# Linear attention: three products and the split of the scores on GpSimd, decays multiplied into the queries in place

## The chip, the cores and the metric

One core of one Trainium2 chip. Five engines matter: TensorE (PE in the profile; PEld is its loading of weights), VectorE (DVE), ScalarE (ACT), GpSimd (POOL), and SyncE (SP), which issues the transfers. The metric is the device time of one execution in microseconds; smaller is better.

## The reference

The kernel computes one layer of a hybrid encoder block on 1024 tokens of width 1024. The part that the change touches is branch A, a gated linear attention that runs in both directions, with 4 heads, keys of 128 and values of 256 elements. For one direction:

```python
b = jnp.cumsum(log_g, axis=3)              # within a chunk of 64 tokens
q_dec = q * jnp.exp(b)
k_inv = k * jnp.exp(-b)
k_tail = k * jnp.exp(b_last - b)
scores = jnp.where(mask, einsum(q_dec, k_inv), 0.0)
o_intra = einsum(scores, v)
chunk_kv = einsum(k_tail, v)
state = exp(b_last) * state + chunk_kv     # from chunk to chunk
o_inter = einsum(q_dec, state_before)
```

The backward direction is the same on flipped sequences, without the diagonal. Both results are added, normalised per head and gated. Branch B is a windowed attention with normalised, rotated keys and queries. Both branches go through output projections, a residual and a SwiGLU layer.

## The kernel before

**Precision.** Large products are made from fp32 operands split in two fp32r parts (a high part and a rest), with three matmuls in place of one. A split is a copy on ScalarE and a subtraction on VectorE (`wh` and `wl` of L70 and L72 for the weights; `kth`, `ktl` for turned keys; `sh`, `sl` for scores).

**Stages.** First come projections made with seven products of blocks in place of eight (to about 332 us), then the linear attention (about 332 to 557 us), the windowed attention (about 557 to 735 us), and then output projections and the feed-forward layer.

**The linear attention.** The tokens are handled in chunks of 128 (eight, c = 0 to 7, for each of four heads), and the gates for two chunks at once (a pair, `pr`). Inside a chunk the powers are counted from its middle (element 63), so that a chunk of 128 needs two numbers a direction (`pr.sm`): the log decay from its border to the middle and from the middle to its other border. The functions:

- `g_gates` (every second slot): loads keys and queries `qk`; TensorE makes the gate logits `z`; ScalarE takes exp, VectorE a minimum, ScalarE a logarithm, VectorE the running sum `cs`; `sm` is taken from it.
- `g_powers` (the slot after): `e` is the running sum counted from the middle; two exponentials on ScalarE turn `e` into the powers and the inverse powers (in the tiles `cs` and `e`); four multiplications on VectorE make the keys `en` (two directions) and the queries `q2` (two directions), 128x256 each.
- `g_scores`, two slots after a chunk's number: TensorE turns the keys (`kt`, split into `kth` and `ktl`) and makes the scores of both directions; a ScalarE copy and a VectorE copy under the mask `tri` join them into `sp`, which VectorE splits into `sh` and `sl`.
- `g_out`, four slots after: TensorE makes the keys-times-values `kv` of both directions; a small exponential on ScalarE makes the decay `dec` from the last chunk's middle to this one's; ScalarE scales the state `pf` by it into `th`; VectorE updates the state; TensorE multiplies the scores with the values and adds the query times `th`.
- `g_back_out` and `g_back`: the backward state walks from the last chunk to the first, with its own small exponential and its own scaled copy `thb` on ScalarE; TensorE multiplies the backward query with `thb`; VectorE adds it to the chunk's output `ob`; then come norm and, in `g_turn`, the turn back and the stores.

**What sets the order.** TensorE's order is written out by hand: a loop over slots calls the functions that are due, and between them `fill` issues a number of matmuls of other projections (12 in most slots, 8 later), which need nothing from the linear attention but weights. The other engines run in an order that a planner makes at compile time from the dependences and its own costs of instructions; each engine then runs its list strictly in order. Tiles come from pools with a fixed number of buffers (`bufs`); a tile's next use waits for the readers of the one before. Results of TensorE that these functions read lie in four buffers named `ch`.

Of the kernel before, what the change touches and what calls it, by code (L numbers as in the profile page):

```python
# [8 lines left out]
F32 = mybir.dt.float32  # L9
# [5 lines left out]
P = 128  # L15
# [15 lines left out]
def body(tc, i, out):  # L31
    nc = tc.nc
    with ExitStack() as root:
# [586 lines left out]
        def gtile(tag, shape=(P, 256), dt=F32, bufs=2):  # L620
            return gt.tile(list(shape), dt, tag=tag, name=nm(tag), bufs=bufs)
# [3 lines left out]
        def g_gates(hd, c):  # L625


            pr = Chunk()
            for j in range(2):
                a = gla[hd, c + j] = Chunk()  # L630
                a.pr, a.j, a.t = pr, j, slice(j * P, (j + 1) * P)
            s, co = c // 4, (c % 4) * P
            for nme in ("q", "k"):
                need((f"{nme}{hd}", s))
            qk = gtile("qk", (P, 2, 256))
            nc.sync.dma_start(out=qk[:, 0], in_=scr[f"q{hd}", s][:, co:co + 256])
            nc.sync.dma_start(out=qk[:, 1], in_=scr[f"k{hd}", s][:, co:co + 256])
            if hd == 0:

                r = rstd[:, c * P:(c + 2) * P]  # L640
                nc.vector.scalar_tensor_tensor(qk[:, 0], qk[:, 0], 128 ** -0.5, r, op0=ALU.mult, op1=ALU.mult)
                nc.vector.tensor_tensor(qk[:, 1], qk[:, 1], r, op=ALU.mult)
            z = chtile((P, 2, 256))
            for d in range(2):
                mm(z[:, d], upS[:, d, hd * P:(hd + 1) * P], lrS[:, c * P:(c + 2) * P], True, True)
            e = gtile("e", (P, 2, 2, P), bufs=1)
            ef = e.rearrange("p d j t -> p (d j t)")
            nc.scalar.activation(ef, z.rearrange("p d t -> p (d t)"), AF.Exp, scale=-1.0)

            nc.vector.tensor_scalar(ef, ef, float(np.expm1(8.0)), None, op0=ALU.min)  # L650
            nc.scalar.activation(ef, ef, AF.Ln, bias=ones[:, 0:1])

            cs = gtile("cs", (P, 2, 2, P), bufs=1)
            csf = cs.rearrange("p d j t -> p (d j t)")
            nc.vector.tensor_tensor_scan(csf, mask.rearrange("p c t -> p (c t)"), ef, 0.0, op0=ALU.mult, op1=ALU.add)  # L655

            pr.qk, pr.e, pr.cs = qk, e, cs
            pr.sm = gtile("sm", (P, 2, 2, 2), bufs=16)
            nc.vector.tensor_scalar(pr.sm, cs[:, :, :, 63:128:64], -1.0 / 16, None, op0=ALU.mult)
            nc.vector.tensor_tensor(pr.sm[:, :, :, 1], pr.sm[:, :, :, 1], pr.sm[:, :, :, 0], op=ALU.subtract)  # L660

        def g_powers(hd, c):

            pr = gla[hd, c].pr
            qk, e, cs = pr.qk, pr.e, pr.cs
            ef, csf = (v.rearrange("p d j t -> p (d j t)") for v in (e, cs))
            nc.vector.tensor_tensor(e[:, 0], cs[:, 0], cs[:, 0, :, 63:64].to_broadcast([P, 2, P]), op=ALU.subtract)
            nc.vector.tensor_tensor(e[:, 1, :, 1:P], cs[:, 1, :, 0:P - 1], cs[:, 1, :, 63:64].to_broadcast([P, 2, P - 1]),
                                    op=ALU.subtract)
            nc.vector.tensor_scalar(e[:, 1, :, 0:1], cs[:, 1, :, 63:64], -1.0, None, op0=ALU.mult)  # L670

            x1 = cs.rearrange("p d j t -> p d (j t)")
            x2 = e.rearrange("p d j t -> p d (j t)")
            nc.scalar.activation(csf, ef, AF.Exp, scale=-1.0 / 16)
            nc.scalar.activation(ef, ef, AF.Exp, scale=1.0 / 16)
            pr.en = gtile("en", (P, 2, 256))
            nc.vector.tensor_tensor(pr.en[:, 0], x2[:, 0], qk[:, 1], op=ALU.mult)
            nc.vector.tensor_tensor(pr.en[:, 1], x1[:, 1], qk[:, 1], op=ALU.mult)
            pr.q2 = (gtile("q2f", bufs=3), gtile(f"q2b{c}", bufs=(3, 2, 2, 1)[c // 2]))
            nc.vector.tensor_tensor(pr.q2[0], x1[:, 0], qk[:, 0], op=ALU.mult)  # L680
            nc.vector.tensor_tensor(pr.q2[1], x2[:, 1], qk[:, 0], op=ALU.mult)

        def g_scores(hd, c):

            a = gla[hd, c]
            a.vh = gtile("vh", dt=FR, bufs=3)
            a.vl = gtile("vl", dt=FR, bufs=3)
            for t, nme in ((a.vh, "vh"), (a.vl, "vl")):
                nc.sync.dma_start(out=t.bitcast(F32), in_=scr[f"{nme}{hd // 2}", c][:, (hd % 2) * 256:(hd % 2) * 256 + 256])
            kt = chtile((P, 2, P))  # L690
            for d in range(2):
                nc.tensor.transpose(kt[:, d], a.pr.en[:, d, a.t], ident)
            a.kth = gtile("kth", (P, 2, P), FR, bufs=3)
            a.ktl = gtile("ktl", (P, 2, P), FR, bufs=3)
            nc.scalar.activation(a.kth, kt, AF.Copy)
            nc.vector.tensor_tensor(a.ktl, kt, a.kth.bitcast(F32), op=ALU.subtract)
            sc = chtile((P, 2, P))
            for d in range(2):
                mm(sc[:, d], a.pr.en[:, d, a.t], a.pr.q2[d][:, a.t], True, True)
            sp = gtile("sp", (P, P))  # L700
            nc.scalar.copy(sp, sc[:, 0])
            nc.vector.copy_predicated(sp, tri, sc[:, 1])
            a.sh = gtile("sh", (P, P), FR, bufs=3)
            a.sl = gtile("sl", (P, P), FR, bufs=3)
            nc.vector.tensor_copy(a.sh, sp)
            nc.vector.tensor_tensor(a.sl, sp, a.sh.bitcast(F32), op=ALU.subtract)

        def g_out(hd, c):

            a = gla[hd, c]  # L710
            kv = chtile((P, 2, 256))
            for d in range(2):
                mm3(kv[:, d], a.kth[:, d], a.ktl[:, d], a.vh, a.vl, True, True)
            a.pf = gtile("pf")
            if c:
                pf = gla[hd, c - 1].pf
                dec = gtile("dec", (P, 1))
                p = gla[hd, c - 1]
                nc.scalar.activation(dec, a.pr.sm[:, 0, a.j, 0:1], AF.Exp, bias=p.pr.sm[:, 0, p.j, 1:2])
                th = gtile("th")  # L720
                nc.scalar.activation(th, pf, AF.Copy, scale=dec[:, 0:1])
                nc.vector.scalar_tensor_tensor(a.pf, pf, dec[:, 0:1], kv[:, 0], op0=ALU.mult, op1=ALU.add)
                a.kb = gtile(f"kb{c}", bufs=2 if c < 5 else 1)
                nc.scalar.copy(a.kb, kv[:, 1])
            else:
                nc.vector.tensor_copy(a.pf, kv[:, 0])
                a.kb = None
            o = chtile((P, 256))
            mm3(o, a.sh, a.sl, a.vh, a.vl, True, c == 0)
            if c:  # L730
                mm(o, a.pr.q2[0][:, a.t], th, False, True)
            a.ob = gtile(f"ob{c}", bufs=2 if c < 5 else 1)
            nc.scalar.copy(a.ob, o)

        def g_back(hd, c):

            a = gla[hd, c]
            if c < NC - 1:
                n = gla[hd, c + 1]
                dec = gtile("decb", (P, 1))  # L740
                nc.scalar.activation(dec, a.pr.sm[:, 1, a.j, 1:2], AF.Exp, bias=n.pr.sm[:, 1, n.j, 0:1])
                a.thb = gtile("thb")
                nc.scalar.activation(a.thb, n.kb, AF.Copy, scale=dec[:, 0:1])
                if c:
                    nc.vector.scalar_tensor_tensor(a.kb, n.kb, dec[:, 0:1], a.kb, op0=ALU.mult, op1=ALU.add)

        def g_back_out(hd, c):
            a = gla[hd, c]
            if c < NC - 1:
                o2 = chtile((P, 256))  # L750
                mm(o2, a.pr.q2[1][:, a.t], a.thb, True, True)
                nc.vector.tensor_tensor(a.ob, a.ob, o2, op=ALU.add)
            if c:
                g_back(hd, c - 1)

            if c % 2:
                a.ss = gtile("oss", (P, 2))
            ss = a.ss if c % 2 else gla[hd, c + 1].ss
            sq = gtile("osq", bufs=1)
            nc.scalar.activation(sq, a.ob, AF.Square, accum_out=ss[:, 1 - c % 2:2 - c % 2])  # L760
            if c % 2 == 0:
                rs = gtile("ors", (P, 2))
                rsqrt(rs, ss, 1.0 / 256, EPS, epst, gt, (P, 2), "on")
                for j, v in enumerate((gla[hd, c + 1].ob, a.ob)):
                    nc.scalar.activation(v, v, AF.Copy, scale=rs[:, j:j + 1])
# [771 lines left out]
```

## Time and profile before

| what | value |
|---|---|
| median of three runs | 1645.5 us (1644.73 to 1645.68) |
| the profiled execution | 1645.61 us, its span 1643.8 us |
| PE busy | 1626.0 us (99%) |
| DVE busy | 1251.4 us (76%) |
| ACT busy | 842.6 us (51%) |
| POOL busy | 76.0 us (5%), all but a few constants in the windowed attention |
| granted clock of TensorE | full speed in all slices |

The page gives the busy time of each engine, then 40 slices of the span, the transfers, the chain of work that ended last, and groups of instructions with their count, busy time and mean duration. Other views list the same for one tile, a stretch of time, or the waits of one engine for another. A matmul's record overlaps the next one's, so the busy share of PE hides a part of short waits.

### The profile page before, as it was taken

How to read it: one execution, taken by the hardware profiler on the slowest of the kernel's cores; microseconds unless marked ns; L12 is line 12 of the kernel's file. 1: busy time of each engine (PE TensorE's matmuls, PEld its weight loads, DVE VectorE, ACT ScalarE, POOL GpSimd, SP SyncE). 2: the span in 40 equal slices, each digit the busy share in tenths (PEclk: the TensorE clock that was granted, in tenths of full speed). 3: DMA queues.
4: the chain of work that ended last, by engine and by line, in shares of the span. 5: the costliest groups of instructions: out<-in, count | busy, mean ns of one | idle time of the engine just before them, and what ended most of it. 6: DMA issues, size and time to landing. Idle time of an engine off the chain costs nothing.

```text
span 1643.8 us, 23281 instructions
## 1 busy us (share of the span) xinstructions
PE 1626.0 (99%) x7588; PEld 1346.0 (82%) x7588; DVE 1251.4 (76%) x2559; ACT 842.6 (51%) x1762; POOL 76.0 (5%) x68
## 2 busy tenths in 40 slices
PE   9999999999999989999999999999999999999999
PEld 7888888888888778888888888888888888888887
DVE  8866665589986598867885678887777778779655
ACT  8622224468998666665554557333333333354442
POOL 0000000000000034540000000000000000000000
PEclk9999999999999999999999999999999999999999
DMA  7554334475554633248765544443334443596433
GB/s 238 176 178 148 115 122 135 173 250 173 179 161 129 191 108 97 77 138 280 225 205 175 168 146 145 140 149 109 109 115 147 142 147 129 177 341 193 149 98 119
DMA packets 168010, 262.91 MB, mean 160 GB/s; under 512 B 19324, under 2 KB 52860, under 8 KB 167888
## 3 DMA queue, kind: packets, MB, share of 16 engines
q1 hardware_dynamic: 167888, 261.42, 49.8%
q8 instruction: 60, 0.98, 0.2%
q14 instruction: 62, 0.51, 0.1%
HBM read 187.93 MB, written 73.42 MB: 159 GB/s over the span
## 4 chain that ended last, share of the span: by engine, by line
PE 84%; DVE 9%; ACT 4%; DMA 2%; issue 1%; POOL 1%; SPq 0%; ACTq 0%; DVEq 0%
PE mm L76 23%; PE mm L306 9%; PE mm L308 9%; PE mm L307 9%; PE mm L1350 7%; PE ch L1350 5%; PE ch L76 4%; PE ch L306 4%; PE ch L308 4%; PE ch L307 4%; PE ch L460 3%; PE mm L460 2%; ACT p L956 1%; DVE wl L72 1%; DVE cs L655 1%
## 5 line engine op out<-in xcount | busy, mean ns | idle before, releaser
L298 ACT ACTIVATE wh<-ws 128x512 fp32r<-128x512 f32 x132 | 83.3, 632 | 195.9 <-PE mm L307 102.2
L70 ACT ACTIVATE wh<-wr 128x512 fp32r<-128x512 f32 x202 | 124.9, 626 | 87.4 <-PE mm L76 54.9
L72 DVE TENSOR_TENSOR wl<-wr,wh 128x512 fp32r<-128x512 f32 x202 | 137.7, 686 | 26.8 <-ACT wh L70 26.4
L299 DVE TENSOR_TENSOR wl<-ws,wh 128x512 fp32r<-128x512 f32 x132 | 90.5, 686 | 22.7 <-ACT wh L298 22.6
L298 ACT ACTIVATE wh<-wr 128x512 fp32r<-128x512 f32 x69 | 43.6, 632 | 124.8 <-issue 49.7
L962 POOL TENSOR_SCALAR p<-p,rd 128x384 f32<-128x384 f32 (+1 forms) x64 | 75.8, 1202 | 657.1 <-DMA qr<-sq 587.2
L298 ACT ACTIVATE wh<-a 128x512 fp32r<-128x512 f32 x64 | 40.5, 633 | 91.4 <-PE ch L1350 42.3
L76 PE MATMUL mm<-wh,xl 128*128 128x512 f32 x192 | 83.1, 433 | 0.0
L76 PE MATMUL mm<-wh,xh 128*128 128x512 f32 x192 | 79.6, 415 | 0.0
L76 PE MATMUL mm<-wl,xh 128*128 128x512 f32 x192 | 79.6, 414 | 0.0
L299 DVE TENSOR_TENSOR wl<-a,wh 128x512 fp32r<-128x512 f32 x64 | 44.2, 691 | 43.1 <-ACT wh L298 42.5
L1350 PE MATMUL mm<-hh,wh 128*128 128x512 f32 x176 | 68.5, 389 | 0.0
L1350 PE MATMUL mm<-hl,wh 128*128 128x512 f32 x176 | 68.5, 389 | 0.0
L1350 PE MATMUL mm<-hh,wl 128*128 128x512 f32 x176 | 68.5, 389 | 0.0
L76 PE MATMUL mm<-xl,wh 128*128 128x512 f32 x160 | 64.5, 403 | 0.1
L76 PE MATMUL mm<-xh,wh 128*128 128x512 f32 x160 | 64.4, 403 | 0.2 <-ACT wh L70 0.2
L76 PE MATMUL mm<-xh,wl 128*128 128x512 f32 x160 | 59.2, 409 | 0.0
L1320 DVE TENSOR_TENSOR hl<-hr,hh 128x512 fp32r<-128x512 f32 x75 | 51.4, 685 | 3.7 <-ACT hh L1319 3.7
L1350 PE MATMUL ch<-hh,wh 128*128 128x512 f32 x132 | 51.3, 389 | 0.0
L1350 PE MATMUL ch<-hl,wh 128*128 128x512 f32 x132 | 51.3, 389 | 0.0
L1350 PE MATMUL ch<-hh,wl 128*128 128x512 f32 x132 | 51.3, 389 | 0.0
L76 PE MATMUL mm<-oah,wh 128*128 128x512 f32 x128 | 50.2, 392 | 0.0
(620 smaller groups left out, 5077.7 us busy)
## 6 DMA issues: line engine op xcount, KB each, us to landing
wr<-in_w_fi_dram SPq DMA_DIRECT2D x102, 256.0 KB
wr<-in_w_f_dram SPq DMA_DIRECT2D x80, 256.0 KB
wr<-in_w_t_dram SPq DMA_DIRECT2D x56, 256.0 KB
B<-c SPq DMA_DIRECT2D x44, 256.0 KB
T<-tx SPq DMA_DIRECT2D x44, 256.0 KB
a<-in_w_fo_dram SPq DMA_DIRECT2D x44, 256.0 KB
hr<-T SPq DMA_DIRECT2D x44, 256.0 KB
wr<-in_w_ob_dram SPq DMA_DIRECT2D x32, 256.0 KB
```

The costliest lines, as they stand in the source:

```text
L70: nc.scalar.activation(h, raw, AF.Copy)
L72: nc.vector.tensor_tensor(l, raw, h.bitcast(F32), op=ALU.subtract)
L76: nc.tensor.matmul(o, a, b, start=start, stop=stop)
L298: nc.scalar.activation(h, src, AF.Copy)
L299: nc.vector.tensor_tensor(l, src, h.bitcast(F32), op=ALU.subtract)
L306: nc.tensor.matmul(o, h[:, c], x[kk][0], start=start and kk == 0, stop=False, skip_group_check=True)
L307: nc.tensor.matmul(o, h[:, c], x[kk][1], start=False, stop=False, skip_group_check=True)
L308: nc.tensor.matmul(o, l[:, c], x[kk][0], start=False, stop=kk == nk - 1, skip_group_check=True)
L460: nc.tensor.matmul(ys[m], a[:, c], b, start=f0, stop=f1, skip_group_check=True)
L962: nc.gpsimd.tensor_scalar(p[:, h, :w], p[:, h, :w], rd[:, h:h + 1], None, op0=ALU.mult)
L1320: nc.vector.tensor_tensor(l, r, h.bitcast(F32), op=ALU.subtract)
L1350: nc.tensor.matmul(ys[m], a[:, c], b, start=f0, stop=f1, skip_group_check=True)
```

## The change

It touches only the linear attention.

- The tiles `cs` and `e` (one buffer each) become the halves of one tile `pw` with two buffers.
- The two keys of a pair are made by one 128x512 multiplication on GpSimd instead of two of 128x256 on VectorE (their order in `en` is swapped, and the readers index accordingly). The two queries are made on GpSimd instead of VectorE.
- The split of the scores (`sh`, a copy, and `sl`, a subtraction) moves from VectorE to GpSimd.
- The decays of a pair are made in `g_powers`: two small additions on VectorE (one, for a head's first pair) and one exponential on ScalarE. The small exponentials in `g_out` and `g_back` go.
- Instead of scaling the state into a copy (`th`, `thb`, on ScalarE), the query is multiplied by the decay in place, on VectorE, after the scores have read it. TensorE then multiplies it with the state itself (`pf`, and the next chunk's `kb`).

```diff
-            e = gtile("e", (P, 2, 2, P), bufs=1)
+            pr.w = gtile("pw", (P, 2, 2, 2, P))
+            cs, e = pr.w[:, 0], pr.w[:, 1]
...
-            cs = gtile("cs", (P, 2, 2, P), bufs=1)
...
+            pr.dec = gtile("dec", (P, 2, 2), bufs=16)
+            nc.vector.tensor_tensor(pr.dec[:, 1], pr.sm[:, :, 1, 0], pr.sm[:, :, 0, 1], op=ALU.add)
+            if c:
+                nc.vector.tensor_tensor(pr.dec[:, 0], pr.sm[:, :, 0, 0], gla[hd, c - 1].pr.sm[:, :, 1, 1], op=ALU.add)
+            dc = pr.dec[:, 0 if c else 1:2]
+            nc.scalar.activation(dc, dc, AF.Exp)
...
-            nc.vector.tensor_tensor(pr.en[:, 0], x2[:, 0], qk[:, 1], op=ALU.mult)
-            nc.vector.tensor_tensor(pr.en[:, 1], x1[:, 1], qk[:, 1], op=ALU.mult)
+            nc.gpsimd.tensor_tensor(pr.en, pr.w.rearrange("p a d j t -> p (a d) (j t)")[:, 1:3],
+                                    qk[:, 1:2].to_broadcast([P, 2, 256]), op=ALU.mult)
...
-            nc.vector.tensor_tensor(pr.q2[0], x1[:, 0], qk[:, 0], op=ALU.mult)
-            nc.vector.tensor_tensor(pr.q2[1], x2[:, 1], qk[:, 0], op=ALU.mult)
+            nc.gpsimd.tensor_tensor(pr.q2[0], x1[:, 0], qk[:, 0], op=ALU.mult)
+            nc.gpsimd.tensor_tensor(pr.q2[1], x2[:, 1], qk[:, 0], op=ALU.mult)
...
-            nc.vector.tensor_copy(a.sh, sp)
-            nc.vector.tensor_tensor(a.sl, sp, a.sh.bitcast(F32), op=ALU.subtract)
+            nc.gpsimd.tensor_copy(a.sh, sp)
+            nc.gpsimd.tensor_tensor(a.sl, sp, a.sh.bitcast(F32), op=ALU.subtract)
...
-                dec = gtile("dec", (P, 1))
-                p = gla[hd, c - 1]
-                nc.scalar.activation(dec, a.pr.sm[:, 0, a.j, 0:1], AF.Exp, bias=p.pr.sm[:, 0, p.j, 1:2])
-                th = gtile("th")
-                nc.scalar.activation(th, pf, AF.Copy, scale=dec[:, 0:1])
-                nc.vector.scalar_tensor_tensor(a.pf, pf, dec[:, 0:1], kv[:, 0], op0=ALU.mult, op1=ALU.add)
+                dec = a.pr.dec[:, a.j, 0:1]
+                q = a.pr.q2[0][:, a.t]
+                nc.vector.tensor_scalar(q, q, dec, None, op0=ALU.mult)
+                nc.vector.scalar_tensor_tensor(a.pf, pf, dec, kv[:, 0], op0=ALU.mult, op1=ALU.add)
...
-                mm(o, a.pr.q2[0][:, a.t], th, False, True)
+                mm(o, q, pf, False, True)
...
-                dec = gtile("decb", (P, 1))
-                nc.scalar.activation(dec, a.pr.sm[:, 1, a.j, 1:2], AF.Exp, bias=n.pr.sm[:, 1, n.j, 0:1])
-                a.thb = gtile("thb")
-                nc.scalar.activation(a.thb, n.kb, AF.Copy, scale=dec[:, 0:1])
+                dec = (n if a.j else a).pr.dec[:, 1 - a.j, 1:2]
+                q = a.pr.q2[1][:, a.t]
+                nc.vector.tensor_scalar(q, q, dec, None, op0=ALU.mult)
+                a.after = n.kb
...
-                mm(o2, a.pr.q2[1][:, a.t], a.thb, True, True)
+                mm(o2, a.pr.q2[1][:, a.t], a.after, True, True)
```

More of the change, by code (lines that the diff above doesn't have):

```diff
@@ L691, in g_scores @@
             for d in range(2):
-                nc.tensor.transpose(kt[:, d], a.pr.en[:, d, a.t], ident)
+                nc.tensor.transpose(kt[:, d], a.pr.en[:, 1 - d, a.t], ident)
             a.kth = gtile("kth", (P, 2, P), FR, bufs=3)
@@ L698, in g_scores @@
             for d in range(2):
-                mm(sc[:, d], a.pr.en[:, d, a.t], a.pr.q2[d][:, a.t], True, True)
+                mm(sc[:, d], a.pr.en[:, 1 - d, a.t], a.pr.q2[d][:, a.t], True, True)
             sp = gtile("sp", (P, P))
@@ L739, in g_back @@
                 n = gla[hd, c + 1]
-                dec = gtile("decb", (P, 1))
-                nc.scalar.activation(dec, a.pr.sm[:, 1, a.j, 1:2], AF.Exp, bias=n.pr.sm[:, 1, n.j, 0:1])
-                a.thb = gtile("thb")
-                nc.scalar.activation(a.thb, n.kb, AF.Copy, scale=dec[:, 0:1])
+                dec = (n if a.j else a).pr.dec[:, 1 - a.j, 1:2]
+                q = a.pr.q2[1][:, a.t]
+                nc.vector.tensor_scalar(q, q, dec, None, op0=ALU.mult)
+                a.after = n.kb
                 if c:
-                    nc.vector.scalar_tensor_tensor(a.kb, n.kb, dec[:, 0:1], a.kb, op0=ALU.mult, op1=ALU.add)
+                    nc.vector.scalar_tensor_tensor(a.kb, n.kb, dec, a.kb, op0=ALU.mult, op1=ALU.add)
         def g_back_out(hd, c):
```

## The prediction

> **What bounds the kernel now.** I read the page's busy times first, then the windows of the stage that is changed, then the waits inside it.
>
> ```profile
> PE 1626.0 (99%) x7588; PEld 1346.0 (82%) x7588; DVE 1251.4 (76%) x2559; ACT 842.6 (51%) x1762; POOL 76.0 (5%) x68
> ```
>
> TensorE is the bound everywhere. In a windows row stand the stretch, its length, and the busy time of PE, PEld, DVE, ACT and POOL:
>
> ```profile
> 332.00:557.00 225.00, 222.56 (x1246) 188.09 (x1245) 184.71 (x612) 192.29 (x556) 0.00 (x0) 1.00 0.57 173
> 350.00:470.00 120.00, 118.56 (x692) 100.90 (x690) 116.10 (x408) 105.46 (x311) 0.00 (x0) 1.00 0.58 174
> ```
>
> In the linear attention (332 to 557 us) TensorE shows 225 - 222.56 = 2.44 us of idle time; its instructions and their order do not change. So all that this change can win is time in which TensorE waits, however much work it takes from the others. DVE is at 97% and ACT at 88% from 350 to 470 us, and their lateness is what TensorE waits for. The waits of the stage for PE and its weight loads (engine, line, what it waited for: us in total, times, longest):
>
> ```profile
> PEld ch L76 <- ACT ob L733: 3.5, 6, 0.9
> PE ch L76 <- ACT ob L733: 1.4, 4, 0.5
> PEld ch L771 <- ACT ob L765: 1.3, 2, 0.9
> PEld ch L771 <- DVE ktl L696: 1.3, 2, 0.7
> PEld ch L76 <- DVE ktl L696: 1.3, 4, 0.5
> PEld ch L76 <- ACT kb L724: 1.1, 3, 0.5
> PE ch L771 <- ACT ob L765: 0.5, 1, 0.5
> PE ch L771 <- DVE ktl L696: 0.4, 2, 0.2
> ```
>
> PE itself waits 4 + 1 + 2 = 7 times, 1.4 + 0.5 + 0.4 = 2.3 us, mostly for ACT to empty a buffer of TensorE's results (L733) or to finish a norm (L765). The counted idle is not all. Here is the first of these waits:
>
> ```profile
> 401.95 0.39 PE L76 MATMUL mm<-wh,xh 128*128 128x512 f32 x1
> 402.18 0.40 PE L76 MATMUL mm<-wl,xh 128*128 128x512 f32 x1
> 403.08 0.50 PE L76 MATMUL ch<-lrS,upS 98*128 98x256 f32 x2 [0.50 <-ACT ob L733]
> ```
>
> Such matmuls start 402.18 - 401.95 = 0.23 us apart; this one is followed after 0.90 us, so 0.67 us are lost where 0.50 are counted. Each wait hides 0.17 us. Lost time: 2.44 + 7 x 0.17 = 3.6 us. Weight loads add up to 3.5 + 1.3 + 1.3 + 1.3 + 1.1 = 8.5 us of waiting, most of it under matmuls still running; that is an upper bound for the loss.
>
> **The change part by part.** What it takes away (line, engine, shapes and count | busy us, mean ns):
>
> ```profile
> L721 ACT ACTIVATE th<-pf,dec 128x256 f32<-128x256 f32 x28 | 14.5, 518 | 0.2
> L743 ACT ACTIVATE thb<-kb,decb 128x256 f32<-128x256 f32 x28 | 14.1, 511 | 1.1 <-PE ch L76 1.1
> L719 ACT ACTIVATE dec<-sm 128x1 f32<-128x1 f32 x16 | 4.9, 303 | 0.2 <-DVE sm L660 0.2
> L741 ACT ACTIVATE decb<-sm 128x1 f32<-128x1 f32 x16 | 4.6, 286 | 0.8 <-DVE sm L660 0.7
> L719 ACT ACTIVATE dec<-sm,sm 128x1 f32<-128x1 f32 x12 | 3.5, 294 | 0.2 <-DVE sm L659 0.2
> L741 ACT ACTIVATE decb<-sm,sm 128x1 f32<-128x1 f32 x12 | 3.5, 291 | 0.1
> L678 DVE TENSOR_TENSOR en<-cs,qk 128x256 f32<-128x256 f32 x16 | 6.8, 422 | 1.6 <-ACT cs L674 1.6
> L681 DVE TENSOR_TENSOR q2b<-e,qk 128x256 f32<-128x256 f32 x16 | 6.7, 421 | 0.0
> L706 DVE TENSOR_TENSOR sl<-sp,sh 128x128 fp32r<-128x128 f32 x32 | 9.2, 288 | 0.3
> L705 DVE CAST sh<-sp 128x128 fp32r<-128x128 f32 x32 | 7.1, 223 | 0.2
> L650 DVE TENSOR_SCALAR e<-e 128x512 f32<-128x512 f32 x16 | 6.8, 423 | 3.4 <-DMA wr<-in_w_t_dram 3.0 <-ACT e L648 0.4
> L659 DVE TENSOR_SCALAR sm<-cs 128x8 f32<-128x8 f32 x16 | 2.6, 166 | 0.0
> L660 DVE TENSOR_TENSOR sm<-sm 128x4 f32<-128x4 f32 x16 | 2.5, 157 | 0.0
> ```
>
> ACT loses 14.5 + 14.1 + 4.9 + 4.6 + 3.5 + 3.5 = 45.1 us and gains 16 exponentials at the 0.30 us of L719, 4.8: net -40 us of 192, from 85% of the stage to 68%.
>
> DVE loses four products a pair (L677 and L680 are like the two shown): 4 x 16 x 0.42 = 27.0, and the splits, 16.3: 43.3 us. It gains 28 additions at 0.157 (L660), 4.4 us, and 56 in-place multiplications of 128x256 by a scalar. No row has that one; on the line between L659 (8 elements, 0.166) and L650 (512, 0.423) it is 0.29, and it is not above the 0.42 of a product of that size. I take 0.29, the same kind of instruction: 16.4 us (23.5 at most). Net -22 us (-15), 1.4 us a pair. None of these lies on TensorE's path by itself; they shorten the lists in which L733, L765 and L696 stand. The decay and the in-place product have two slots between the scores and their use. Backward, TensorE now waits for `kb` itself rather than for `thb`, one ACT step less.
>
> POOL gains seven instructions a pair: one product of 512, two of 256, two copies and two subtractions of 128. The only rows are of another operation:
>
> ```profile
> L962 POOL TENSOR_SCALAR p<-p,rd 128x384 f32<-128x384 f32 x48 | 59.8, 1263 | 57.6 <-DVE rd L960 22.0 <-ACT ph L976 14.7 <-ACT sob L987 8.2
> L962 POOL TENSOR_SCALAR p<-p,rd 128x256 f32<-128x256 f32 x16 | 16.1, 1020 | 599.5 <-DMA qr<-sq 587.2 <-DVE rd L960 5.8 <-ACT sob L987 3.5
> ```
>
> They give 1.90 ns an element and 0.53 us a start: 1.51 us for 512, 1.02 for 256, 0.78 for 128. A pair: 1.51 + 2 x 1.02 + 4 x 0.78 = 6.7 us. If a second operand doubles the part per element: 2.48 + 2 x 1.51 + 2 x (0.78 + 1.02) = 9.1. If POOL were as fast as DVE: 4 x 0.42 + 2 x 0.51 = 2.7. I take 6.7, the nearest rows. What hides it is the distance from the second exponential to TensorE's first use of the keys; the tightest of the 16 pairs, and the first and last gate matmul:
>
> ```profile
> 350.41 0.62 ACT L675 ACTIVATE e<-e 128x512 f32<-128x512 f32 x1
> 355.21 0.38 PE L692 MATMUL ch<-ident,en 128*128 128x128 f32 x2
> ...
> 331.98 0.40 PE L76 MATMUL ch<-lrS,upS 98*128 98x256 f32 x2
> ...
> 496.55 0.41 PE L76 MATMUL ch<-lrS,upS 98*128 98x256 f32 x2
> ```
>
> From 351.03 to 355.21 are 4.2 us; the three products take 1.51 + 2.04 = 3.6 us there (5.5 at the high price, too late by about a microsecond). A pair comes every (496.55 - 331.98) / 15 = 10.97 us, so POOL is 61% busy (83% at the high price). The scores' split has two slots until its use. So I put POOL's work at nothing on TensorE's path. The second buffer of the powers removes a wait that no row shows as TensorE's: nothing.
>
> [...] No row here shows a two-input operation on POOL.
>
> **Sum:** 1645.6 (the profiled execution, 0.1 above the median of the runs) - 3.6 = **1642.0 us**.
>
> **The rivals.**
>
> *The late keys* (slower). POOL runs its list in order; if two splits stand ahead of the products and the second operand costs, the backward query is ready 1.8 + 5.5 = 7.3 us after the exponential, where the tightest pair has 4.2, and about 0.4 more until that query is read. TensorE then stands 2.7 us. A stand also moves the next pair's deadline, so half of it counts; over some seven tight pairs that is 9 us: **1651**. It decides from 4.6 us on. For it: POOL's collisions with DVE, below. At its extreme, with 0.49 us of collision for each of seven instructions, 9.1 + 3.4 = 12.5 us exceeds the 10.97 of a pair, and POOL is the bound: 15 x 1.5 = 23 us.
>
> *DVE held by POOL* (slower). If an instruction of DVE with two operands in SBUF, or one by a scalar, had to stand until POOL's ends, some 12 a pair would wait, each with a chance of 0.61, for half of the 0.95 us of a POOL instruction: 3.5 us. From 350 to 470 us DVE then has 116.1 x 10.97/120 - 1.4 + 3.5 = 12.7 us a pair for 10.97, for 11 pairs: 19 us, **1661**. The rows speak against it:
>
> ```profile
> 626.81 4.92 POOL L962 TENSOR_SCALAR p<-p,rd 128x384 f32<-128x384 f32 x4 [6.25 <-DVE rd L960]
> 629.81 0.69 DVE L916 TENSOR_TENSOR qn<-qr,qA 128x512 f32<-128x512 f32 x1
> ```
>
> And the durations (ns, min/median/max) of a later burst:
>
> ```profile
> L962 POOL TENSOR_SCALAR p<-p,rd x4: 1247/1248/1740, 692.3 to 695.9; 128x384 f32<-128x384 f32 x4
> ```
>
> A two-operand product of DVE ran inside a burst of POOL at its usual 0.69 us; in another burst one POOL instruction took 1740 ns instead of 1247. So where they collide, POOL pays. [...]
>
> *Nothing lands*: the planner's new lists put L733 and L765 as late as before: **1645.5**. ACT's load falling by a fifth speaks against it.
>
> *The next stage starts earlier too*. DVE waits 2.5 us for a table at the start of the windowed attention, and tables wait for stores of this stage:
>
> ```profile
> DVE qA L859 <- DMA sink<-in_sink_dram: 2.5, 1, 2.5
> ```
>
> Tiles move with the new sizes; if that goes, 1642.0 - 2.5 = **1639.5**. Nothing says that it will.
>
> **How the numbers follow.** The forecast has 0.56, with its own range 1640.5 to 1644; nothing lands 0.14; the next stage 0.08; late keys 0.14; DVE held 0.08. The range 1638.5 to 1652 leaves out DVE held and the worse half of late keys. A measurement of this kernel tells 0.2%, 3.3 us, from no change, so faster begins at 1642.2: three fifths of the forecast's chance (0.34) and the earlier start (0.08), 0.42. The same: the rest of the forecast's (0.21) and nothing lands, 0.35. Slower: 0.23, the two rivals and a sliver of the forecast.
>
> **What would show it.** Right: PE's idle time in the stage below 1 us, ACT near 68%, waits for L733 and L765 gone, POOL near 107 us more in all. Wrong: PE waiting for POOL at the turn of the keys or the scores; `wl` or `e` of DVE longer than their 0.69 and 0.42 us or DVE idle behind POOL; a POOL product of 512 above 2.5 us.

## The result and the profile after

The changed kernel takes 1667.7 us (median of four runs, 1667.0 to 1668.9) against 1645.1 us of the kernel before (1644.6 to 1645.7): the ratio is 1.0136, with a 95% interval of 1.0123 to 1.0149. It is 22 us slower, where 3.6 us less were forecast, and above the range of 1638.5 to 1652.

The page of the changed kernel, first part, and its windows of the linear attention, which now ends 20 us later (the columns are those of the windows before: the stretch, its length, then PE, PEld, DVE, ACT and POOL):

```profile
PE 1634.3 (98%) x7588; PEld 1349.5 (81%) x7588; DVE 1261.1 (76%) x2515; ACT 815.9 (49%) x1666; POOL 152.3 (9%) x180
```

```profile
332.00:577.00 245.00, 229.61 (x1248) 189.42 (x1248) 194.27 (x568) 165.18 (x461) 76.32 (x112) 0.99 0.52 159
577.00:757.00 180.00, 170.16 (x899) 141.70 (x898) 147.59 (x477) 113.43 (x299) 75.77 (x64) 0.99 0.37 113
```

TensorE runs the same instructions and stands for 245 - 229.6 = 15.4 us of this stage, where it was 2.4. That is 13 of the 20 us by which the stage is longer. The other 7 show as longer busy time for the same work (229.6 against 222.6); how much of them is hidden behind waits and how much is the granted clock, 0.99 here and 1.00 before, was not worked out. The windowed attention behind it, moved as a whole, has about as much idle time as before (9.8 us in 180, 9.5 in 178). ACT fell, 192 to 165 us. DVE, which was to fall by 22, rose from 185 to 194 us with 44 instructions fewer. The longest waits of PE in the stage (us in total, times, longest):

```profile
PE ch L76 <- ACT kb L729: 6.6, 8, 2.8
PE ch L76 <- DVE ob L757: 4.0, 4, 1.4
PE ch L76 <- DVE ktl L703: 1.8, 6, 0.7
PE ch L76 <- ACT ob L738: 1.6, 1, 1.6
```

No row has PE waiting for POOL. PE waits for buffers of its own results, which ACT and DVE empty late. The longest single wait, 2.80 us, in the order of time. Lines are left out where the three dots stand:

```profile
395.44 0.74 POOL L687 TENSOR_TENSOR q2f<-pw,qk 128x256 f32<-128x256 f32 x1 [5.29 <-ACT pw L681]
395.48 0.73 DVE L101 TENSOR_SCALAR rt<-ss 128x2 f32<-128x2 f32 x1
...
396.92 1.28 POOL L684 TENSOR_TENSOR en<-pw,qk 128x512 f32<-128x512 f32 x1
397.01 2.07 DVE L798 SCALAR_TENSOR_TENSOR qn<-kvr,rs,kg 128x128 f32<-128x128 f32 x2
...
398.17 0.77 POOL L688 TENSOR_TENSOR q2b<-pw,qk 128x256 f32<-128x256 f32 x1
399.11 0.29 DVE L801 TENSOR_TENSOR sq<-qn,sink 128x128 f32<-128x128 f32 x1
...
399.52 0.47 DVE L727 SCALAR_TENSOR_TENSOR pf<-pf,dec,ch 128x256 f32<-128x256 f32 x1
...
400.03 0.37 ACT L729 COPY kb<-ch 128x256 f32<-128x256 f32 x1 [1.86 <-DVE pf L727]
...
400.46 0.50 PE L76 MATMUL ch<-lrS,upS 98*128 98x256 f32 x2 [2.80 <-ACT kb L729]
```

This is one wait of many, but it shows how the loss comes about. DVE's L101 works on two elements a partition and takes 0.73 us: it ends 0.03 us after POOL's product `q2f`. The next two `qn` (L798, 0.35 us each in the kernel before) take 2.07 us together; taken singly, the first ends 0.15 us after POOL's `en`, the second 0.15 us after `q2b`. They belong to the windowed attention's keys, which nobody needs yet. But behind them in DVE's list stands the update of the state `pf`; ACT's copy `kb` waits for `pf`, and PE waits 2.80 us for the buffer that `kb` empties.

The groups of DVE that tell this apart, of the changed kernel and then of the one before (count | busy us, mean ns):

```profile
L72 DVE TENSOR_TENSOR wl<-wr,wh 128x512 fp32r<-128x512 f32 x48 | 37.6, 789 | 17.9 <-ACT wh L70 17.7
L703 DVE TENSOR_TENSOR ktl<-ch,kth 128x256 fp32r<-128x256 f32 x32 | 13.4, 418 | 7.1 <-ACT kth L702 7.1
L801 DVE TENSOR_TENSOR sq<-qn,sink 128x128 f32<-128x128 f32 x8 | 3.5, 435 | 0.2
L101 DVE TENSOR_SCALAR rt<-ss 128x2 f32<-128x2 f32 x8 | 2.6, 324 | 0.1
```

```profile
L72 DVE TENSOR_TENSOR wl<-wr,wh 128x512 fp32r<-128x512 f32 x48 | 32.7, 687 | 11.4 <-ACT wh L70 11.4
L696 DVE TENSOR_TENSOR ktl<-ch,kth 128x256 fp32r<-128x256 f32 x32 | 13.4, 419 | 6.1 <-ACT kth L695 5.8
L796 DVE TENSOR_TENSOR sq<-qn,sink 128x128 f32<-128x128 f32 x8 | 2.3, 287 | 0.1
L101 DVE TENSOR_SCALAR rt<-ss 128x2 f32<-128x2 f32 x8 | 1.3, 164 | 0.0
```

Products of two operands in SBUF (`wl`, `sq`) and operations by a scalar (L101) became longer in the mean, `sq` by half, L101 by double. `ktl`, which reads one operand from TensorE's results (`ch`) and one from SBUF (where the kernel's other tiles lie), kept its 0.42 us.

The mean hides that only some of the `wl` are held, and these all in one way. Here is one of them:

```profile
385.34 1.34 POOL L684 TENSOR_TENSOR en<-pw,qk 128x512 f32<-128x512 f32 x1
...
385.84 1.39 DVE L72 TENSOR_TENSOR wl<-wr,wh 128x512 fp32r<-128x512 f32 x1
```

It starts inside POOL's `en` and ends 0.55 us after it. Of the 48 `wl` that start in the stage, 14 start inside a GpSimd instruction of two operands. Each of them ends 0.55 us after that instruction, however much of it was left (0.17 to 0.97 us), and takes 1.04 us in the mean. The other 34 take 0.69 us each, as before. So what a held `wl` loses depends on how much of GpSimd's instruction is left when it starts: with 0.17 us left it took 0.71 us, with 0.97 left 1.52.

### The profile page after: what moved, and what is told of

Same layout as the page of the kernel before. It is cut to its first block, busy times and chain, and to the rows that moved or that the text cites. A ratio compares the mean times of both kernels' runs of the same rounds, so it can differ in the third digit from the quotient of the medians.

```text
span 1665.2 us, 23402 instructions
## 1 busy us (share of the span) xinstructions
PE 1634.3 (98%) x7588; PEld 1349.5 (81%) x7588; DVE 1261.1 (76%) x2515; ACT 815.9 (49%) x1666; POOL 152.3 (9%) x180
## 4 chain that ended last, share of the span: by engine, by line
PE 82%; DVE 10%; ACT 4%; DMA 1%; issue 1%; POOL 1%; SPq 0%; ACTq 0%; DVEq 0%
PE mm L76 22%; PE mm L306 9%; PE mm L307 9%; PE mm L308 9%; PE mm L1355 7%; PE ch L1355 5%; PE ch L76 4%; PE ch L307 4%; PE ch L306 4%; PE ch L308 4%; PE ch L460 3%; PE mm L460 2%; DVE wl L72 1%; ACT p L961 1%; DVE pw L655 1%
## 5 line engine op out<-in xcount | busy, mean ns | idle before, releaser
L72 DVE TENSOR_TENSOR wl<-wr,wh 128x512 fp32r<-128x512 f32 x202 | 142.4, 711 | 33.0 <-ACT wh L70 32.6
```

What stands on the lines that cost most here:

```text
L72: nc.vector.tensor_tensor(l, raw, h.bitcast(F32), op=ALU.subtract)
```

## The experiments

The theory after the result, **held DVE**: an instruction of GpSimd that reads two operands holds DVE's instructions that work from SBUF until it ends; urgent instructions of DVE stand behind the held ones, and TensorE behind these. The rivals: **late keys** (POOL's results come too late for TensorE), and **decays in place** (the new chain through the decay's exponential and the in-place products is longer).

### The parts of the change, one by one

Decays alone, products and splits back on VectorE:

```diff
-            nc.gpsimd.tensor_tensor(pr.en, ...)          # and both q2, sh, sl
+            nc.vector.tensor_tensor(...)                 # as before the change
```

> The changed kernel with the products and the splits back on VectorE; the decays in place and the two buffers of the powers stay, GpSimd does nothing in this stage. Held DVE (GpSimd's two-operand instructions make VectorE's stand): without GpSimd the loss goes and the forecast's gain is left, 1641 to 1643.5 us. Late keys (GpSimd's list is too slow for TensorE): the same. Decays in place (the in-place products and the decay's exponential ahead of the powers lengthen the chain): still slow, 1655 to 1668.

The two GpSimd parts with the old decays (`dec`, `th`, `decb`, `thb` on ScalarE as before):

> The changed kernel with the old decays back (small exponentials and scaled copies of the state on ScalarE); products and splits stay on GpSimd. Held DVE: the stretch of VectorE stays and ScalarE has its 40 us again, so as slow as the whole change or slower, 1663 to 1675. Late keys: the same. Decays in place: fast, 1641 to 1647.

The decays and the splits on GpSimd, products on VectorE:

> The changed kernel with the products back on VectorE, only the splits of the scores on GpSimd (29 of its 78 us in this stage). Held DVE: the loss shrinks with GpSimd's time, 22 x 29/78 = 8 us, on top of VectorE's 27 us of products being back: 1650 to 1660. Late keys: nothing is late, 1641 to 1645. Decays in place: 1655 to 1668.

The decays and the products on GpSimd, splits on VectorE:

> The changed kernel with the splits back on VectorE, only the products on GpSimd (48 of its 78 us). Held DVE: 22 x 48/78 = 14 us are left, 1653 to 1663. Late keys: nearly the whole loss, since the products are what TensorE would wait for, 1660 to 1668, less a few us since no split stands ahead of them. Decays in place: 1655 to 1668.

Measured, beside 1645.7 us of the kernel before:

| kernel | us | ratio, 95% interval |
|---|---|---|
| decays alone | 1646.5 | 1.0006 (0.9996 to 1.0015) |
| GpSimd parts alone | 1662.1 | 1.0100 (1.0085 to 1.0115) |
| decays, splits on GpSimd | 1654.0 | 1.0051 (1.0036 to 1.0066) |
| decays, products on GpSimd | 1662.3 | 1.0103 (1.0086 to 1.0120) |

The decays alone cost nothing, so that rival falls. They also bring nothing, though 2 to 5 us of gain were expected of this run; more on that below. With the decays in place, the loss comes with GpSimd, from either part: 8 us with the splits, 16 with the products, 22 with both. Late keys would have left the splits alone at no cost; the time of the products alone fits both theories, but TensorE has no wait for POOL there either.

The GpSimd parts alone missed their expectation by a microsecond on the low side. They cost 16 us, and the decays, free by themselves, cost 5.6 more on top of them (1667.7 against 1662.1). A likely reason is that the decays bring 56 in-place products to DVE, and these are held too: 0.29 us each with the decays alone, 0.33 and 0.41 in the whole change. With the GpSimd parts alone DVE is far from full:

```profile
332.00:572.00 240.00, 227.14 (x1245) 189.25 (x1244) 175.41 (x484) 191.59 (x555) 76.53 (x112) 0.99 0.54 162
```

DVE is busy for 175 of 240 us, less than the 185 of 225 before (in its densest part, 350 to 470 us, 103 of 120 us, before 116), and TensorE still stands for 12.9 us. So it isn't the sum of DVE's work that costs, but which instruction is held, and what stands behind it.

### The contention by itself

Further GpSimd instructions were added to the kernel before, with results that nobody reads. The order of PE, ACT and DVE stayed the same to the instruction. The code is shortened; `mk` is a constant mask in SBUF:

```diff
+            nc.gpsimd.tensor_tensor(junk, en, mk, op=ALU.mult)           # 512, a pair
+            nc.gpsimd.tensor_tensor(junk[:, 0:256], q2[d], mk[:, 0:256], op=ALU.mult)   # two, a pair
...
+            nc.gpsimd.tensor_tensor(junk[:, 0:128], ktl[:, 0], mk[:, 0:128], op=ALU.mult)   # two, a chunk
```

> The kernel before, with 7 further GpSimd instructions a pair whose results nobody reads: a product of two operands of 512 elements behind the keys, two of 256 behind the queries, two of 128 behind each chunk's turned keys. The lists of the other engines stay the same to the instruction. Held DVE: VectorE's instructions with two operands in SBUF stretch beside GpSimd and TensorE waits, with no gain anywhere: 1655 to 1670 us, since VectorE has its full load of before. Late keys: nobody waits for these products, so 1645 to 1647.

The same with one operand and a scalar:

```diff
+            nc.gpsimd.tensor_scalar(junk, en, ones[:, 0:1], None, op0=ALU.mult)          # and so on
```

> As the run with further products of two operands, but each is a multiplication of one operand by a scalar a partition, the form that GpSimd runs in the windowed attention. Held DVE by any GpSimd instruction that reads SBUF: 1655 to 1670, as that run. Held DVE only where GpSimd reads two operands (which would explain why the windowed attention showed VectorE at its usual pace): 1645 to 1650. Late keys: 1645 to 1647.

The same with fills:

> As the run with further products, but GpSimd only fills a tile with zeros (two fills of 512 and four of 256 a pair, two of 256 a chunk, each group behind a copy of one column): it writes and hardly reads. Held DVE through what GpSimd reads: 1645 to 1648. Held DVE through any GpSimd instruction: stretched in proportion to the busy time of POOL, 1650 to 1665. Late keys: 1645 to 1647.

| added to the kernel before | us | ratio, 95% interval |
|---|---|---|
| two operands | 1681.1 | 1.0215 (1.0198 to 1.0232) |
| one operand and a scalar | 1652.3 | 1.0042 (1.0027 to 1.0057) |
| fills | 1647.5 | 1.0011 (1.0001 to 1.0020) |

The windows of the stage of these three, in this order:

```profile
332.00:591.00 259.00, 233.05 (x1247) 187.44 (x1247) 222.21 (x612) 194.22 (x557) 91.19 (x112) 1.00 0.50 151
```

```profile
332.00:564.00 232.00, 225.54 (x1245) 187.70 (x1244) 194.15 (x612) 192.23 (x555) 118.88 (x112) 1.00 0.55 168
```

```profile
332.00:559.00 227.00, 223.72 (x1248) 188.45 (x1247) 186.54 (x612) 191.83 (x555) 78.53 (x208) 1.00 0.57 173
```

The same 612 instructions of DVE took 185 us before, 222 beside two-operand instructions, 194 beside one-operand ones and 187 beside fills. The time follows: 37.5, 9.4 and 1.8 us more of DVE, 35, 7 and 2 us more in all. Nobody waits for these results, so late keys can't be the cause. (In the one-operand run DVE waits once, 1.3 us, for an added instruction; in the other two never.) POOL's busy time isn't the measure either: the one-operand run has the most of it (119 us) and a fifth of the loss. What differs between the three runs is the kind of instruction that POOL runs. The two-operand run went past its expected 1655 to 1670, the one-operand run is between its two cases, and the fills are within the 1645 to 1648 of holding by what POOL reads.

The groups of DVE in the run with two operands, against 687, 419, 421 and 223 ns before:

```profile
L72 DVE TENSOR_TENSOR wl<-wr,wh 128x512 fp32r<-128x512 f32 x48 | 40.7, 853 | 11.0 <-ACT wh L70 11.0
L701 DVE TENSOR_TENSOR ktl<-ch,kth 128x256 fp32r<-128x256 f32 x32 | 13.3, 414 | 6.1 <-ACT kth L700 6.1
L682 DVE TENSOR_TENSOR q2b<-e,qk 128x256 f32<-128x256 f32 x16 | 11.0, 686 | 0.0
L710 DVE CAST sh<-sp 128x128 fp32r<-128x128 f32 x32 | 10.8, 338 | 0.2
```

Again the instruction that reads `ch` is untouched, and those with both operands in SBUF stretch. So does the copy `sh`, which has only one. Of the 48 `wl` in the stage 18 start inside an added product: 14 end 0.55 us after it, three start in its last 0.06 us and lose nothing, and one takes its usual time although 1.0 us was left. The run with one operand and a scalar differs:

```profile
361.94 2.13 POOL L684 TENSOR_SCALAR junk<-en,ones 128x512 f32<-128x512 f32 x1 [1.56 <-DVE en L678]
...
362.03 0.68 DVE L72 TENSOR_TENSOR wl<-wr,wh 128x512 fp32r<-128x512 f32 x1
...
363.49 0.61 DVE L101 TENSOR_SCALAR rt<-ss 128x2 f32<-128x2 f32 x1
...
363.62 0.54 DVE L710 CAST sh<-sp 128x128 fp32r<-128x128 f32 x1
```

Here `wl` starts inside POOL's instruction and keeps its 0.68 us; POOL's takes 2.13 us, where its kind takes 1.79 in the mean. L101 and the copy `sh`, usually 0.16 and 0.22 us, last until POOL's instruction has ended. Of 48 `wl` in the stage 26 start inside such an instruction, and they take 0.70 us in the mean. Beside the fills, `wl` takes 684 ns and `sl` 286 in the mean, as in the kernel before, but `sh` 256 and the two groups of L101 250 and 224 (166 and 164 before).

The number of operands that POOL reads is not the whole of it. Beside two operands the `wl` that started inside were held (14 of 14 in the changed kernel, 14 of 18 beside the added products), beside one operand and a scalar the 26 kept their pace; but in the changed kernel two of the three `qn` that start inside GpSimd's copy `sh`, which has one operand, end 0.14 us after it, nearly as those inside products do (0.15 us), and the third keeps its 0.28 us. Why the operation by a scalar differs is open.

### The splits, half by half

Only the copy `sh` on GpSimd, and only the subtraction `sl`, both with the decays in place:

> The run with the decays alone, with only the copy that makes the first half of the score's split on GpSimd (one operand, 14 of the 29 us of the run with both halves there). Held DVE by two-operand instructions of GpSimd mostly: 1645 to 1648. Held DVE by GpSimd's time whatever it reads: half of that run's 8 us, 1649 to 1652.

> The run with the decays alone, with only the subtraction that makes the second half of the score's split on GpSimd (two operands, 16 of the 29 us). Held DVE by two-operand instructions mostly: nearly all of the 8 us that both halves cost, 1650 to 1655. Held DVE by GpSimd's time whatever it reads: half of it, 1649 to 1652.

The copy alone takes 1654.4 us (1.0053, 1.0036 to 1.0070), the subtraction alone 1650.8 (1.0030, 1.0019 to 1.0042). The copy misses both expectations. One of its waits is new:

```profile
DVE sl L713 <- POOL sh L712: 6.0, 30, 0.5
```

With one half on each engine, DVE itself waits for POOL, 30 times and 6.0 us in all, in the middle of its list. That is a wait that the whole change does not have, since both halves go to POOL there. So this run has a handoff between two engines in a full list besides, and it can't tell what the copy holds. The subtraction alone, 4 us more than the decays alone, lies in both of its ranges, 1650 to 1655 and 1649 to 1652, and decides nothing. Its DVE rows show few held instructions, and how its loss divides between holding and a new order of the lists is not settled.

### Where the forecast's gain is

If relieving ScalarE brings nothing, what does TensorE wait for? ScalarE was given the in-place multiplications and the copy `sh`, with nothing on GpSimd:

```diff
-                nc.vector.tensor_scalar(q, q, dec, None, op0=ALU.mult)      # both places
+                nc.scalar.activation(q, q, AF.Copy, scale=dec)
-            nc.vector.tensor_copy(a.sh, sp)
+            nc.scalar.activation(a.sh, sp, AF.Copy)
```

> The run with the decays alone (nothing on GpSimd in this stage), with the in-place multiplications by the decay and the first half of the score's split on ScalarE instead of VectorE. If VectorE's list is what TensorE waits for once ScalarE is relieved (it took 10 us more in that run while ScalarE lost 28), this takes some 20 us from VectorE and leaves ScalarE below its load before, and TensorE's lost 3 to 4 us go: 1641.5 to 1644. If VectorE's load is not it, 1645 to 1647.

It takes 1645.2 us (0.9998, 0.9988 to 1.0007): no change that can be told, so VectorE's load by itself is not what TensorE waits for. Then one line was moved: ACT's copy `kb` ahead of DVE's update of `pf`. Both read one buffer of results, and the one issued second is seen waiting for the other: in the whole change `kb` waits 19 times for `pf`, 16.4 us in all; with the line moved there, `pf` waits 6 times for `kb`, 3.2 us.

```diff
+                a.kb = gtile(f"kb{c}", bufs=2 if c < 5 else 1)
+                nc.scalar.copy(a.kb, kv[:, 1])
                 nc.vector.scalar_tensor_tensor(a.pf, pf, dec, kv[:, 0], op0=ALU.mult, op1=ALU.add)
-                a.kb = gtile(f"kb{c}", bufs=2 if c < 5 else 1)
-                nc.scalar.copy(a.kb, kv[:, 1])
```

> The run in which ScalarE takes the in-place multiplications and half of the split, with one line moved: the copy of the backward half of the keys-times-values (kb, ScalarE) is issued ahead of the update of the forward state (pf, VectorE). Both read one buffer of TensorE's results, and in the kernel before the copy waits for the update, so the buffer comes free only behind VectorE's list. If that chain is why relieving ScalarE brought nothing, the waits for kb go, TensorE's idle time in the stage falls to about 1 us, and the run takes 1641.5 to 1644 us. If the waits only move on to the next reader, 1644 to 1646.5.

It takes 1644.0 us (0.9990, 0.9981 to 0.9999): 1.6 us less than the kernel before by the ratio, with an interval that just leaves out no change. That is where its two cases meet. The windows of the decays alone, of ScalarE's run before the line was moved, and of this run:

```profile
332.00:557.00 225.00, 222.60 (x1245) 187.89 (x1245) 194.78 (x696) 164.20 (x460) 0.00 (x0) 1.00 0.57 173
```

```profile
332.00:557.00 225.00, 223.07 (x1243) 187.14 (x1242) 181.94 (x608) 182.91 (x547) 0.00 (x0) 1.00 0.56 172
```

```profile
332.00:557.00 225.00, 223.11 (x1253) 189.61 (x1252) 182.93 (x609) 183.27 (x549) 0.00 (x0) 1.00 0.58 175
```

TensorE stands 2.40 us with the decays alone, as before, although ACT has 28 us less; 1.93 us in ScalarE's run; and 1.89 us here, where about 1 was expected. So the counted idle time does not show the gain. The distance from the first to the last gate matmul does: 163.6 us here (331.89 to 495.45), 165.7 before the line was moved (332.34 to 498.01), 164.6 in the kernel before (331.98 to 496.55). The longest waits of PE with the decays alone, and then those of this run, from which the rows for `kb` are gone:

```profile
PE ch L76 <- DVE ob L757: 0.7, 1, 0.7
PE ch L76 <- ACT kb L729: 0.5, 1, 0.5
PE ch L76 <- DVE ktl L703: 0.3, 1, 0.3
```

```profile
PE ch L76 <- DVE ob L757: 0.7, 1, 0.7
PE ch L76 <- DVE ktl L703: 0.5, 2, 0.3
PE ch L76 <- ACT ob L738: 0.4, 2, 0.2
PE ch L776 <- ACT ob L770: 0.3, 1, 0.3
```

The same line moved in the whole change:

> The whole change, with one line moved as in the run that copies kb first: the copy of the backward keys-times-values on ScalarE is issued ahead of the update of the forward state on VectorE, so that it no longer waits for VectorE's list. Held DVE: VectorE's held instructions reach TensorE through whatever urgent instruction stands behind them; the way over kb (6.6 of TensorE's counted waits of the changed kernel) goes, the ways over the output's sum and the keys' split stay: 1654 to 1663 us. If the loss had been VectorE's sum of work and not such standing behind, nothing changes: 1666 to 1669.

It takes 1664.4 us (1.0113, 1.0097 to 1.0130), 3 us less than the whole change, 1.4 above the range of held DVE and below the 1666 of its rival. The waits for `kb` are gone there too; TensorE waits for other buffers instead:

```profile
PE ch L76 <- ACT ob L738: 3.7, 4, 1.7
PE ch L76 <- DVE ob L757: 2.9, 2, 1.8
PE ch L76 <- DVE pf L729: 2.1, 3, 1.1
PE ch L76 <- DVE ktl L703: 2.0, 5, 0.5
```

So `kb` was one way among several by which a held list of DVE reaches TensorE, and closing one of them wins little.

## Why the prediction was wrong

**What bounds the kernel.** Right, and it held in every run: TensorE is the bound, and where the time grows, its idle time grows (in the stage 2.4 us before, 15.4 with 22 us more in all, 26.0 with 35 more). The ceiling on the gain was not passed; the best version has 1.6 us of the 3.6.

**The step that failed** is the reading of the row at 629.81: "So where they collide, POOL pays." That burst of POOL was a one-operand operation by a scalar, the only form the trace had, and for that form it holds for instructions like `wl`: with one operand and a scalar added, `wl` kept its pace and POOL's instruction took 2.13 us against 1.79 in the mean. The change puts two-operand products there, and for them it fails: in the changed kernel each of the 14 `wl` that start inside such an instruction waits for its end. With the lists of the other engines unchanged, two operands cost 35 us and one operand 7. From the one form I judged the other, gave held DVE 0.08, and so left the holding out of the sum. The sign that was named for it came true: `wl` took 0.79 us, not 0.69.

**DVE held by POOL, its size.** The rival said 1661, the result is 1667.7. It was priced as a sum: DVE's list overflows the 10.97 us of a pair, over the full part of the stage, on top of the gain. The GpSimd parts alone show that no overflow is needed: with DVE busy 175 of 240 us, 16 us were lost. A held instruction costs what stands behind it, whatever the mean load is. The holding itself was priced too high: against the usual time of its kind, DVE's instructions of the stage took some 26 us more in all, 1.6 us a pair, where the rival had 3.5. And there was no gain to start from. So a result 7 us from the rival's does not mean that its sum was nearly right.

**The relief of ACT, 3.6 us.** Not found: the decays alone took 1646.5. ACT lost 45 us of records and gained 3 (its 16 exponentials took 0.20 us, not 0.30), and showed 28 us less busy time, since records of consecutive instructions overlap and the sum of their durations counts the overlap twice (in the kernel before, ACT's 556 records of the stage add up to 238.6 us, where 192.3 are busy). More to the point, TensorE's waits moved, mostly from ACT's row L733 to DVE's rows and to `kb`: the idle time was 2.44 us before and 2.40 then. The step that failed here is to take the engine that came last in a wait for its cause. The rows fit a buffer that is read in turn by two engines, where the next reader was as late; what holds the remaining 2 us is not shown.

**DVE's terms.** The removed 43.3 us stand. The in-place products are of 128x128, not 128x256 as I had them; alone they take 0.29 us, the price taken for the wrong size, and with holding 0.33 and 0.41 in the mean. Against the predicted 22 us less, DVE has 10 us more (194.3 against 184.7).

**POOL's terms.** The products and splits took less than the 6.7 us a pair:

```profile
L684 POOL TENSOR_TENSOR en<-pw,qk 128x512 f32<-128x512 f32 x16 | 21.1, 1317 | 2.4 <-ACT pw L682 1.8 <-PE ch L776 0.3
L713 POOL TENSOR_TENSOR sl<-sp,sh 128x128 fp32r<-128x128 f32 x32 | 15.8, 495 | 2.2
L688 POOL TENSOR_TENSOR q2b<-pw,qk 128x256 f32<-128x256 f32 x16 | 14.3, 894 | 0.0
L712 POOL CAST sh<-sp 128x128 fp32r<-128x128 f32 x32 | 13.6, 426 | 86.8 <-DVE sp L709 57.7 <-DVE pw L670 10.4 <-DVE sm L660 6.2
L687 POOL TENSOR_TENSOR q2f<-pw,qk 128x256 f32<-128x256 f32 x16 | 13.0, 814 | 373.2 <-ACT dec L677 338.7 <-ACT pw L681 23.3 <-DVE wl L72 11.3
```

(21.1 + 15.8 + 14.3 + 13.6 + 13.0) / 16 = 4.9 us a pair. They were hidden, as forecast: no wait of TensorE for POOL, and late keys did not happen. The engine was cheap by its own time and dear by what it did to another.

**The next stage starts earlier** did not happen either; it moved as a whole.

## What to carry to other kernels

A move to GpSimd is priced by the instructions of VectorE that will run beside it, not by GpSimd's free time (here it was busy for 76 of 245 us, and the kernel lost 22): count VectorE's instructions with both operands in SBUF, and the copies and operations by a scalar in it, and ask what urgent work stands behind each in its list. A row of one kind of GpSimd instruction says little about another (7 us lost beside one operand and a scalar, 35 beside two operands); the cheap test is to add such instructions with results that nobody reads. And when the last waiter of a shared buffer is relieved, look who reads it next before a gain is booked.

## What the runs showed of the hardware

- In the changed kernel the 14 `wl` on VectorE that started inside a GpSimd instruction of two operands all ended 0.55 us after it (0.69 us alone), with 0.17 to 0.97 us of it left; beside the added products 14 of 18 did. A two-element operation by a scalar, 0.16 us alone, took 0.73 and ended 0.03 us after it.
- Instructions of VectorE that read one operand from TensorE's results kept their time in the changed kernel: `ktl` 418 ns in the mean against 419, `ob` 414 against 417.
- The loss went by what GpSimd ran: with the same other lists, 91 us of two-operand instructions cost 35 us, 119 us of one-operand ones 7, and fills with a few short copies (79 us) 2.
- Beside GpSimd's operations by a scalar, VectorE's subtraction `wl` of two operands kept its time (26 of them: 0.70 us in the mean), and GpSimd's instruction around one of them took 2.13 us (1.79 in the mean); a copy and a small operation by a scalar on VectorE lasted until it ended (0.22 to 0.54, 0.16 to 0.61 us).
- Beside fills and a few short copies on GpSimd, VectorE's subtraction `wl` of two operands kept its time (684 ns against 687), and its copy `sh` did not (256 against 223).
- A product of two operands took GpSimd less time than one operand by a scalar a partition: for 128x256 the shortest took 0.73 us (the changed kernel) against 0.92 (the windowed attention before), for 128x512 the mean was 1.32 against 1.79 in the run with added one-operand instructions.
